# Attention scores over 128 contraction rows, one operand kept per head in tiles whose other 64 rows are zero

## The chip, the cores and the metric

The kernel runs on one core of one Trainium2 chip. Its metric is the device time of one execution in microseconds (us), of which the median of several runs is taken. The engines are named as in the profile: PE (matrix products; PEld is its loading of the stationary operand), DVE (vector), ACT (activation functions and copies), POOL (general vector work beside DVE) and SP (which issues most DMAs).

## The reference

Two layers of a decoder trunk over 512 tokens of 1024 features. Layer 0 mixes with attention, layer 1 with a gated delta rule; each is followed by a gated feed-forward part. The change lies in layer 0, where 8 "moba" heads (softmax) and 8 stick-breaking heads of 64 features share one input projection:

```python
proj = h @ w_in
qa, ka, va, qb, kb, vb = (t.reshape(B, T, -1, HEAD_DIM) for t in jnp.split(proj, cuts, axis=-1))
qa = partial_rope(qa, positions)
ka = partial_rope(ka, positions)
# moba heads: with 512 tokens and blocks of 256 this is causal attention
s = einsum('bhqd,bhkd->bhqk', q, k) * dh ** -0.5;  p = softmax(where(causal, s, -inf));  o = p @ v
# stick-breaking heads
z = einsum('bhqd,bhkd->bhqk', q, k) * dh ** -0.5
log_1m = where(strictly_causal, log_sigmoid(-z), 0)
w = exp(log_sigmoid(z) + reverse_cumsum(log_1m) - log_1m);  o = w @ v
```

## The kernel before

Activations lie with features on the 128 partitions and tokens on the free axis. Every product of float32 numbers is made from two rounded parts, a high one and a low one (`h` and `l` at the end of a tile's name): `split` makes the high part by a copy (on ACT, or POOL for some weights) and the low part by a subtraction (DVE), and a product is three matmuls, high by high, high by low, low by high.

One 128-row projection holds two heads of 64 features, a *pair*: head 0 in partitions 0 to 63, head 1 in 64 to 127. There are four pairs; of each pair `finish` makes `qa`, `ka` (scaled, turned by the rotary tables: a shuffle on DVE, a product with `S` on POOL, two DVE operations, then `split`), `qb` and `kb`. The work of a pair is done head by head, `moba` and `stick` in turn, so there are eight units of work. In a unit each of `moba` and `stick` makes four blocks of scores, of 128, 256, 384 and 512 columns, each by one call of `qk3`:

```python
PE.matmul(ps, kh[rs, ks], qh[rs, qs], start=True, stop=False)
PE.matmul(ps, kh[rs, ks], ql[rs, qs], start=False, stop=False)
PE.matmul(ps[:, at], e.identb, mask, start=False, stop=False)
steps[-1].append(PE.matmul(ps, kl[rs, ks], qh[rs, qs], start=False, stop=True).ins)
```

`rs` is the head's 64 partitions, so the three score matmuls contract over 64 rows; the mask in bf16 contracts over 128. `moba` passes q where this text has k and the other way round, so its stationary operand is `qa`; that of `stick` is `kb`. Behind the scores of `moba` come a maximum, an exponential, a scaling, four transposes on PE, a split, and the product with v (`pv_out`); behind those of `stick` three ACT functions, a split, products with triangular constants (`ntri`, `nones`), an exponential, a split on POOL, and `pv_out`.

PE takes its work in a fixed order. While the heads of a pair go on, the projections of the next pair (`proj`, and `vproj` for v) fill PE between their steps: `spread` hands each part of a projection a score matmul behind which it is issued. The order on each engine is found when the kernel is built, and each engine then keeps it.

The attention begins with a stage in which the first projections go along with the arrival of the normed input, chunk by chunk (the loop over `k`): loads of two blocks of `ada_w` (tile `aw`, from the pool `rtmp`, 6 buffers), their product with `cond` on DVE, the norm, one weight load (`raw`), its split, and 24 matmuls. The rotary tables are made in it on POOL. In the attention 24 more products `aw` run on POOL (`AENG`), each followed by a sum on ACT; they hang on nothing but their loads and two buffers. The pool `sq0` of `start()` holds the squares of the input before that loop.

Of the kernel before, what the change touches and what calls it, by code (L numbers as in the profile page):

```python
# [8 lines left out]
F32 = mybir.dt.float32  # L9
# [8 lines left out]
T = 512  # L18
# [112 lines left out]
def build(nc, tc, I, O):  # L131
# [3 lines left out]
    with ctx:  # L135
# [40 lines left out]
        crow = apool.tile([1, D], F32, name="crow")  # L176
        nc.scalar.dma_start(crow, I["c"])
        load_x(xctx.enter_context(pool("xp0", "right")), I["x"], nc.sync)
# [74 lines left out]
        # all weights in the order of their use; the loads and splits run ahead of it  # L253
# [12 lines left out]
        def fetch():  # L266
# [3 lines left out]
            if keep == "h":  # L270
                # in the place of h, which is used no more
# [71 lines left out]
        def start():  # L343
            """cond, and rstd of the first norm."""
# [45 lines left out]
        def out_proj(chunk_w, o, layer, gate, nsplit, after, order=None, between=None, halves=HALVES, keep=False):  # L390
            """x += gate * (w^T o), the last chunks by halves of the tokens; after(half) follows each half."""
# [23 lines left out]
        def halves_first(keys, banks, hs, keep):  # L415
            """Products of some chunks of weights by halves of the tokens, into banks."""
# [93 lines left out]
def attention(e, x0ctx):  # L510
    nc, tc, V, G, A, PE, I = e.nc, e.tc, e.V, e.G, e.A, e.PE, e.I
    from contextlib import ExitStack
    with ExitStack() as ctx:
        p1 = ctx.enter_context(e.pool("at1"))
        # rotary tables
# [8 lines left out]
        def rotary():  # L524
            """cos and -sin, sin of the angles: one frequency and 32 positions to a partition, then spread."""
# [42 lines left out]
        # v by kind and pair of heads; a pair's outputs take the place of the v of the pair before  # L568
# [6 lines left out]
        ctx2 = ExitStack()  # L575
        qk = ctx2.enter_context(e.pool("qk"))
        fin = ctx2.enter_context(e.pool("afin"))

        def finish(ps, name, scale, rope):
            h = qk.tile([128, T], F32R, name=name + "h", bufs=1)  # L580
            l = qk.tile([128, T], F32R, name=name + "l", bufs=1)
            if rope:
                q = fin.tile([128, T], F32, name="rq", bufs=2)
                A.activation(q, ps, AF.Copy, scale=scale)
                sw = fin.tile([128, T], F32, name="rs", bufs=1)
                V.stream_shuffle(sw, q, swap)
                G.tensor_tensor(sw, sw, S, op=OP.mult)
                V.tensor_tensor(q, q, C, op=OP.mult)
                V.tensor_tensor(q, q, sw, op=OP.add)
                e.split(q, h, l)  # L590
            elif scale != 1.0:
                A.activation(h, ps, AF.Copy, scale=scale)
                V.scalar_tensor_tensor(l, ps, scale, h.bitcast(F32), op0=OP.mult, op1=OP.subtract)
            else:
                e.split(ps, h, l)
            return h, l

        KINDS = (("qa", 0.125, True), ("ka", 1.0, True), ("qb", 0.125, False), ("kb", 1.0, False))

        # the first projections go along with the arrival of h, chunk of features by chunk  # L600
        with e.psum_pool("start") as sp, e.pool("rtmp") as tmp:
            pq = [sp.tile([128, T], F32, name=f"pq{i}") if i < 1 else e.mm_tile() for i in range(4)]
            pv = [sp.tile([128, T], F32, name=f"pv{i}") for i in range(4)]
            for k in range(KC):
                for comp in (1, 0):
                    with tc.issue_after(first[0]):
                        e.ada(0, comp, k, tmp, 6)
                    e.ada_fin1(0, comp, e.gmix if comp == 1 else None, k)
                e.ahead[0] = AHEAD if k == KC - 1 else 0
                with tc.issue_after(first[1]):  # L610
                    wh, wl = e.load_w(("attn_first", k))
                ins = e.norm_h(FULL, 0, 0, 1, hs, (k,))
                if k == 0:
                    first = (ins.ins, first[1])
                xh, xl = hs[k]
                a, z = k == 0, k == KC - 1
                if k == ROT:
                  with tc.issue_after(e.pins[0]):
                    nc.sync.dma_start(e.call, I["consts"])
                    rotary()  # L620
                for i in range(4):
                    PE.matmul(pq[i], wh[:, i], xh, start=a, stop=False)
                    PE.matmul(pq[i], wh[:, i], xl, start=False, stop=False)
                    PE.matmul(pq[i], wl[:, i], xh, start=False, stop=z)
                vwh = wh[:, 4:].rearrange("p a b -> p (a b)")
                vwl = wl[:, 4:].rearrange("p a b -> p (a b)")
                for c in range(4):
# [4 lines left out]
            with tc.issue_after(sin[0].ins):  # L632
                e.act_set()
# [635 lines left out]
```

## Time and profile before

| | |
|---|---|
| three runs | 1464.26, 1464.52 (median), 1466.06 us |
| profiled execution, span from its first to its last instruction | 1463.8 us |
| busy share of the span | PE 97%, PEld 81%, DVE 60%, ACT 40%, POOL 27% |
| first loop over `k` | about 18 to 71 us |
| attention units, from the first score product on | 86.8 to about 312 us |
| feed-forward of layer 0, delta rule, feed-forward of layer 1 | the rest |

What lies around the span is not measured apart; the median of the runs stands 0.7 us above the span. A matmul's end is modelled in the profile, so PE reads as busy almost everywhere; what it costs is read from the distance between the starts of one matmul and the next. "Busy" on the other engines can be taken as it stands.

### The profile page before, as it was taken

Reading aid. Unit: us, or ns where it says so; the run is one execution under the profiler, and the core shown is the slowest. Engines: PE = TensorE matmul, PEld = TensorE weight load, DVE = VectorE, ACT = ScalarE, POOL = GpSimd, SP = SyncE. Lnnn points to the kernel's source line nnn. Section 1 sums busy time; section 2 is a strip of 40 time slices with the busy share of each in tenths; the row PEclk is TensorE's granted clock in tenths of the full one; section 3 lists DMA queues with packets and bytes.
Section 4 is the critical chain, followed back from the end, with each engine's and each line's share of the span. In section 5 each row is a group of like instructions: output and inputs, shape, how many; then the busy total and the mean of one; then the engine's idle time right before and its main releaser. Section 6 shows DMA issues by size and latency. Waiting matters only on the chain.

```text
span 1463.8 us, 19775 instructions
## 1 busy us (share of the span) xinstructions
PE 1416.0 (97%) x7610; PEld 1188.0 (81%) x7610; DVE 879.6 (60%) x1408; ACT 581.6 (40%) x1133; POOL 395.4 (27%) x360
## 2 busy tenths in 40 slices
PE   8889999999999999999999999999999999999997
PEld 4677677769888888888978777999998888888887
DVE  7588875656566666523677888757784343333233
ACT  4466555664322222222446643345563222222222
POOL 2868833212211111001334644432112000000010
PEclk9999999999999999999999999999999999999999
DMA  9444420123266776633632223223262323233332
GB/s 371 149 159 140 155 71 16 44 85 106 83 235 216 247 237 216 197 110 115 186 95 76 68 74 104 80 78 115 91 206 65 101 94 95 100 101 94 90 96 80
DMA packets 57007, 184.44 MB, mean 126 GB/s; under 512 B 6761, under 2 KB 11113, under 8 KB 56914
## 3 DMA queue, kind: packets, MB, share of 16 engines
q1 hardware_dynamic: 55104, 179.91, 37.7%
q0 software_dynamic: 656, 2.23, 0.7%
q8 instruction: 59, 0.97, 0.3%
q10 hardware_dynamic: 1154, 1.05, 0.2%
q14 instruction: 34, 0.28, 0.1%
HBM read 177.88 MB, written 5.29 MB: 125 GB/s over the span
## 4 chain that ended last, share of the span: by engine, by line
PE 66%; DVE 6%; ACT 2%; DMA 2%; issue 2%; POOL 1%; DVEq 0%; ACTq 0%; POOLq 0%
PE mm L309 18%; PE mm L310 18%; PE mm L311 18%; PE mm L1076 1%; PE mm L1077 1%; PE mm L1075 1%; DMA vp<-dr 1%; DVE vp L972 1%; PE f L309 1%; PE f L310 1%; DVE wl L250 1%; PE f L311 1%; PE bank L910 1%; DVE sq L374 1%; DMA raw<-in_ffn_in_dram 1%
## 5 line engine op out<-in xcount | busy, mean ns | idle before, releaser
L245 ACT ACTIVATE wh<-raw 128x1024 fp32r<-128x1024 f32 (+1 forms) x199 | 206.7, 1040 | 516.6 <-PE mm L310 384.8
L250 DVE TENSOR_TENSOR wl<-raw,wh 128x1024 fp32r<-128x1024 f32 (+1 forms) x205 | 270.1, 1319 | 213.6 <-ACT wh L245 200.1
L309 PE MATMUL mm<-hh,wh 128*128 128x512 f32 (+1 forms) x776 | 295.7, 381 | 2.4 <-DVE acc L863 2.4
L311 PE MATMUL mm<-hh,wl 128*128 128x512 f32 (+1 forms) x776 | 291.5, 377 | 1.2 <-DVE wl L250 1.2
L310 PE MATMUL mm<-hl,wh 128*128 128x512 f32 (+1 forms) x776 | 292.3, 377 | 0.0
L309 PEld LDWEIGHTS mm<-hh,wh 128*128 128x128 f32 x776 | 147.4, 190 | 30.7 <-issue 2.8
L311 PEld LDWEIGHTS mm<-hh,wl 128*128 128x128 f32 x776 | 147.4, 190 | 27.5 <-DVE wl L250 1.8
L310 PEld LDWEIGHTS mm<-hl,wh 128*128 128x128 f32 x776 | 147.5, 190 | 24.1
L247 POOL TENSOR_SCALAR ah<-ac 128x512 fp32r<-128x512 f32 x36 | 40.6, 1129 | 336.8 <-DVE ac L471 336.8
L311 PE MATMUL mm<-ah,wl 128*128 128x512 f32 (+1 forms) x354 | 126.4, 357 | 1.2 <-DVE wl L250 1.2
L309 PE MATMUL mm<-ah,wh 128*128 128x512 f32 (+1 forms) x354 | 126.3, 357 | 0.1
L310 PE MATMUL mm<-al,wh 128*128 128x512 f32 (+1 forms) x354 | 126.0, 356 | 0.0
L309 PE MATMUL mm<-h1h,wh 128*128 128x512 f32 x320 | 124.5, 389 | 0.0
L310 PE MATMUL mm<-h1l,wh 128*128 128x512 f32 x320 | 124.5, 389 | 0.0
L311 PE MATMUL mm<-h1h,wl 128*128 128x512 f32 x320 | 124.5, 389 | 0.0
L471 DVE TENSOR_TENSOR ac<-sg,mm 128x512 f32<-128x512 f32 x40 | 27.5, 688 | 129.1 <-PE mm L311 129.1
L213 DVE CUSTOM_DVE_ANT_0 aw<-aw,cond 128x1024 f32<-128x1024 f32 x72 | 94.7, 1339 | 6.1 <-DMA aw<-in_ada_w_dram 6.0
L329 POOL TENSOR_TENSOR ssq<-ssq,sq 128x512 f32<-128x512 f32 x14 | 22.1, 1577 | 210.3 <-ACT sq L325 210.3
L311 PEld LDWEIGHTS mm<-ah,wl 128*128 128x128 f32 x354 | 66.9, 189 | 11.1 <-DVE wl L250 1.6
L309 PEld LDWEIGHTS mm<-ah,wh 128*128 128x128 f32 x354 | 66.8, 189 | 10.4 <-issue 0.5
L310 PEld LDWEIGHTS mm<-al,wh 128*128 128x128 f32 x354 | 66.9, 189 | 9.4 <-issue 0.2
L310 PEld LDWEIGHTS mm<-h1l,wh 128*128 128x128 f32 x320 | 60.1, 188 | 12.5
(403 smaller groups left out, 2805.1 us busy)
## 6 DMA issues: line engine op xcount, KB each, us to landing
aw<-in_ada_w_dram SPq DMA_DIRECT2D x96, 512.0 KB
raw<-in_ffn_in_dram SPq DMA_DIRECT2D x88, 512.0 KB
raw<-in_ffn_out_dram SPq DMA_DIRECT2D x36, 512.0 KB
raw<-in_gdn_in_dram SPq DMA_DIRECT2D x26, 512.0 KB
raw<-in_gdn_z_dram SPq DMA_DIRECT2D x16, 512.0 KB
raw<-in_gdn_out_dram SPq DMA_DIRECT2D x16, 512.0 KB
raw<-in_ffn_out_dram SPq DMA_DIRECT2D x18, 384.0 KB
raw<-in_attn_in_dram SPq DMA_DIRECT2D x12, 512.0 KB
```

Source lines behind the costliest of these rows:

```text
L213: return V.tensor_tensor_reduce(w, w, cond, 1.0, 0.0, OP.mult, OP.add, mod[:, j:j + 1])
L245: ins = A.activation(h, src, AF.Copy)
L247: G.tensor_scalar(h, src, 1.0, 1.0, op0=OP.mult, op1=OP.mult)
L250: (G if eng == "p" else V).tensor_tensor(l, src, h.bitcast(F32), op=OP.subtract)
L309: PE.matmul(ps, wh[k][:, 0], xh[:, cs], start=first and k == order[0], stop=False)
L310: PE.matmul(ps, wh[k][:, 0], xl[:, cs], start=False, stop=False)
L311: PE.matmul(ps, wl[k][:, 0], xh[:, cs], start=False, stop=last and k == order[-1])
L329: eng.tensor_tensor(ssq[:, cs], ssq[:, cs], sq[:, cs], op=OP.add)
L374: ins = V.scalar_tensor_tensor(t[:, cs], x, modcol(layer, scale, k), rstd[:, cs], op0=OP.mult, op1=OP.mult)
L471: ins = V.tensor_tensor(ac, sg, pu, op=OP.mult)
L910: PE.matmul(ps[:, c], lhs[:, cs], rhs[:, cs], start=True, stop=True)
L972: V.tensor_tensor(DV[:, :m, m:], DV[:, :m, m:], d, op=OP.subtract)
```

## The change

`qa` and `kb`, the two stationary operands of the score products, are kept in tiles of their own for each head. A tile has 128 rows; 64 of them hold the head, the other 64 are set to zero once by POOL, eight tiles in all. The score products then read all 128 rows of both operands: the other head's rows of the moving side meet zeros. `finish` splits `qa` and `kb` in two halves of 64 rows (`finish_apart`), two copies and two subtractions where there was one of each. To make room, the pools `qk` and `fin` are opened after `rtmp` is closed, so `rtmp` now lies where `sq0` was; `crow` goes into the pool of the input; and `w` of `stick` takes one of the three buffers `sq`.

```diff
-        crow = apool.tile([1, D], F32, name="crow")
+        xp0 = xctx.enter_context(pool("xp0", "right"))
+        crow = xp0.tile([1, D], F32, name="crow")
...
         ctx2 = ExitStack()
-        qk = ctx2.enter_context(e.pool("qk"))
-        fin = ctx2.enter_context(e.pool("afin"))
...
-        with e.psum_pool("start") as sp, e.pool("rtmp") as tmp:
+        with e.psum_pool("start") as sp:
             pq = [sp.tile([128, T], F32, name=f"pq{i}") if i < 1 else e.mm_tile() for i in range(4)]
             pv = [sp.tile([128, T], F32, name=f"pv{i}") for i in range(4)]
+            with e.pool("rtmp") as tmp:
+                for k in range(KC):
...
+            qk = ctx2.enter_context(e.pool("qk"))
+            fin = ctx2.enter_context(e.pool("afin"))
+            apart = {}
+            for name in ("qa", "kb"):
+                for head in range(2):
+                    apart[name, head] = [qk.tile([128, T], F32R, name=f"{name}{part}{head}", bufs=1) for part in "hl"]
+                    for t in apart[name, head]:
+                        G.memset(t[64 * (1 - head):64 * (2 - head)].bitcast(F32), 0.0)
+
+            def finish_apart(src, name, scale):
+                for head in range(2):
+                    rs = slice(64 * head, 64 * head + 64)
+                    h, l = (t[rs] for t in apart[name, head])
+                    e.split(src[rs], h, l)
+                return [apart[name, head] for head in range(2)]
...
+                if (name, 0) in apart and not rope:
+                    return finish_apart(ps, name, scale)
...
+                    if (name, 0) in apart:
+                        return finish_apart(q, name, scale)
                     e.split(q, h, l)
...
-            PE.matmul(ps, kh[rs, ks], qh[rs, qs], start=True, stop=False)
-            PE.matmul(ps, kh[rs, ks], ql[rs, qs], start=False, stop=False)
+            PE.matmul(ps, kh[:, ks], qh[:, qs], start=True, stop=False)
+            PE.matmul(ps, kh[:, ks], ql[:, qs], start=False, stop=False)
             PE.matmul(ps[:, at], e.identb, mask, start=False, stop=False)
-            steps[-1].append(PE.matmul(ps, kl[rs, ks], qh[rs, qs], start=False, stop=True).ins)
+            steps[-1].append(PE.matmul(ps, kl[:, ks], qh[:, qs], start=False, stop=True).ins)
...
-                qk3(s[:, :n], q, qs, k, slice(0, n), rs, qs, causal)
+                qk3(s[:, :n], q[h], qs, k, slice(0, n), qs, causal)
...
-                w = work.tile([128, T], F32, name="w", tag="w", bufs=2)
+                w = e.wpool.tile([128, T], F32, name="sq", tag="sq", bufs=3)
```

The built order moves too, on every engine up to the end of the attention; behind it all five engines have the rows that they had. Three places matter below.

SP, the first loads behind those of the input (`call` is the table of constants). Before:

```order
L208 DMA aw<-in_ada_w_dram 128x1024 x2
L269 DMA raw<-in_attn_first_dram 128x1024
L208 DMA aw<-in_ada_w_dram 128x1024 x2
L269 DMA raw<-in_attn_first_dram 128x1024
L208 DMA aw<-in_ada_w_dram 128x1024 x2
L269 DMA raw<-in_attn_first_dram 128x1024
L619 DMA call<-in_consts_dram 128x1025
```

and now:

```order
L270 DMA raw<-in_attn_first_dram 128x1024 x3
L599 DMA call<-in_consts_dram 128x1025
L209 DMA aw<-in_ada_w_dram 128x1024 x6
L270 DMA raw<-in_attn_first_dram 128x1024
```

Three weight loads and the constants have moved ahead of the first `aw`, which now waits for PE to have read the squares in whose place it lies.

POOL, behind the making of the rotary tables (`rs` is the rotary product of `qa`, then of `ka`, of the first pair). Before:

```order
L210 TENSOR_TENSOR aw<-aw,cond 128x1024 x2
L587 TENSOR_TENSOR rs<-rs,S 128x512
L210 TENSOR_TENSOR aw<-aw,cond 128x1024 x2
L587 TENSOR_TENSOR rs<-rs,S 128x512
L210 TENSOR_TENSOR aw<-aw,cond 128x1024 x3
```

and now, behind two `aw` products as before:

```order
L623 MEMSET qah_611 64x512
L623 MEMSET qal_612 64x512
L623 MEMSET qah_615 64x512
L623 MEMSET qal_616 64x512
L623 MEMSET kbh_619 64x512
L623 MEMSET kbl_620 64x512
L623 MEMSET kbh_623 64x512
L623 MEMSET kbl_624 64x512
L211 TENSOR_TENSOR aw<-aw,cond 128x1024 x2
L644 TENSOR_TENSOR rs<-rs,S 128x512
L211 TENSOR_TENSOR aw<-aw,cond 128x1024
L644 TENSOR_TENSOR rs<-rs,S 128x512
```

Eight fillings with zeros and two `aw` products have come ahead of the first rotary product.

ACT, at the end of the first loop, where `qa`, `ka`, `qb` and `kb` of the first pair are read out of PSUM (two `rq`, `qbh`, `kbh`). Before:

```order
L245 ACTIVATE wh<-raw 128x1024
L211 ACTIVATE aw,mod<-aw 128x1024 x2
L245 ACTIVATE wh<-raw 128x1024
L584 ACTIVATE rq<-pq_206 128x512
L584 ACTIVATE rq<-mm 128x512
L592 ACTIVATE qbh<-mm 128x512
```

and now:

```order
L246 ACTIVATE wh<-raw 128x1024
L212 ACTIVATE aw,mod<-aw 128x1024 x2
L246 ACTIVATE wh<-raw 128x1024 x2
L641 ACTIVATE rq<-pq_197 128x512
L212 ACTIVATE aw,mod<-aw 128x1024
L641 ACTIVATE rq<-mm 128x512
L651 ACTIVATE qbh<-mm 128x512
```

One more weight copy stands ahead of the first read, and the sum of a third `aw` product between the first read and the second.

## Rows read from the trace of the kernel before

**Rows 1.** The page: the span, and the busy time, share and number of instructions of each engine, and what the DMA engines moved in each of 40 equal slices of the span (36.6 us each).

```profile
span 1463.8 us, 19775 instructions
PE 1416.0 (97%) x7610; PEld 1188.0 (81%) x7610; DVE 879.6 (60%) x1408; ACT 581.6 (40%) x1133; POOL 395.4 (27%) x360
...
GB/s 371 149 159 140 155 71 16 44 85 106 83 235 216 247 237 216 197 110 115 186 95 76 68 74 104 80 78 115 91 206 65 101 94 95 100 101 94 90 96 80
```

**Rows 2.** Busy time by stretch: start and end of the stretch, its length, then busy time and number of instructions of PE, PEld, DVE, ACT, POOL, the granted clock of PE as a share of 2.4 GHz, the DMA share and GB/s.

```profile
72.00:87.00 15.00, 11.18 (x74) 10.53 (x74) 14.97 (x33) 9.07 (x30) 9.48 (x5) 0.89 0.53 187
87.00:189.00 102.00, 98.14 (x506) 73.95 (x506) 87.00 (x120) 66.11 (x162) 81.68 (x51) 1.00 0.46 150
189.00:302.00 113.00, 113.00 (x540) 81.52 (x538) 72.52 (x144) 64.88 (x157) 32.53 (x39) 1.00 0.10 33
```

**Rows 3.** PE in order of time (start and duration in us, line, tiles, contraction rows * stationary columns, shape of the moving side): a score product of 128 columns, one of 512, and what stands before and behind them.

```profile
224.07 0.39 PE L754 MATMUL z<-ssl,ntri 128*128 128x512 f32 x1
224.38 0.32 PE L697 MATMUL z<-qbh,kbh 64*128 64x128 f32 x1
224.55 0.27 PE L698 MATMUL z<-qbl,kbh 64*128 64x128 f32 x1
224.75 0.23 PE L699 MATMUL z<-strictT,identb 128*128 128x128 bf16 x1
224.91 0.32 PE L700 MATMUL z<-qbh,kbl 64*128 64x128 f32 x1
225.16 0.50 PE L309 MATMUL mm<-hh,wh 128*128 128x512 f32 x1
...
226.41 0.40 PE L310 MATMUL mm<-hl,wh 128*128 128x512 f32 x1
226.74 0.50 PE L697 MATMUL s<-kah,qah 64*128 64x512 f32 x1
227.08 0.39 PE L698 MATMUL s<-kal,qah 64*128 64x512 f32 x1
227.40 0.23 PE L699 MATMUL s<-causal,identb 128*128 128x128 bf16 x1
227.56 0.49 PE L700 MATMUL s<-kah,qal 64*128 64x512 f32 x1
227.99 0.50 PE L309 MATMUL mm<-hh,wh 128*128 128x512 f32 x1
```

**Rows 4.** The same view a little earlier: matmuls of 128 contraction rows one behind the other, of 512, 384, 256 and 128 columns.

```profile
222.80 0.39 PE L311 MATMUL mm<-hh,wl 128*128 128x512 f32 x1
223.03 0.34 PE L754 MATMUL z<-ssh,nones 128*128 128x384 f32 x1
223.21 0.33 PE L754 MATMUL z<-ssl,nones 128*128 128x384 f32 x1
223.38 0.28 PE L754 MATMUL z<-ssh,nones 128*128 128x256 f32 x1
223.50 0.28 PE L754 MATMUL z<-ssl,nones 128*128 128x256 f32 x1
223.61 0.22 PE L754 MATMUL z<-ssh,nones 128*128 128x128 f32 x1
223.67 0.27 PE L754 MATMUL z<-ssl,nones 128*128 128x128 f32 x1
223.78 0.45 PE L754 MATMUL z<-ssh,ntri 128*128 128x512 f32 x1
```

**Rows 5.** The instructions of line 697 (the first matmul of every score product) in the stretch 87 to 189: number, shortest, median and longest duration in ns, first and last start, shapes.

```profile
L697 PE MATMUL s<-kah,qah x14: 302/384/497, 86.8 to 187.4; 64*128 64x128 f32 x4, 64*128 64x256 f32 x4, 64*128 64x384 f32 x3, 64*128 64x512 f32 x3
L697 PE MATMUL z<-qbh,kbh x12: 271/409/497, 87.5 to 180.3; 64*128 64x128 f32 x3, 64*128 64x256 f32 x3, 64*128 64x384 f32 x3, 64*128 64x512 f32 x3
```

**Rows 6.** Groups of instructions by line in the stretch 86 to 189 (number | busy us, mean ns of one | idle before): a split of 64 rows by 512 columns, on ACT and on DVE.

```profile
L245 ACT ACTIVATE ah-1_174<-o 64x512 fp32r<-64x512 f32 x2 | 1.2, 594 | 0.7 <-PE o L690 0.6
L250 DVE TENSOR_TENSOR bl-1_185<-o,bh-1_184 64x512 fp32r<-64x512 f32 x2 | 1.4, 686 | 0.0
```

**Rows 7.** POOL: the one filling of a tile of 512 columns (line 518, durations in ns), then its instructions in order of time between 63 and 87 us.

```profile
L518 POOL MEMSET C<- x1: 543/543/543, 2.2 to 2.2; 128x512 f32 x1
...
63.28 5.71 POOL L210 TENSOR_TENSOR aw<-aw,cond 128x1024 f32<-128x1024 f32 x2
73.13 1.78 POOL L587 TENSOR_TENSOR rs<-rs,S 128x512 f32<-128x512 f32 x1 [4.14 <-DMA aw<-in_ada_w_dram]
80.01 2.27 POOL L587 TENSOR_TENSOR rs<-rs,S 128x512 f32<-128x512 f32 x1
```

**Rows 8.** ACT and PE in order of time at the end of the first loop and before the first score product (idle time before, and what ended it, in brackets).

```profile
69.02 1.06 ACT L211 ACTIVATE aw<-aw 128x1024 f32<-128x1024 f32 x1 [2.18 <-POOL aw L210]
71.50 0.59 ACT L584 ACTIVATE rq<-mm 128x512 f32<-128x512 f32 x1
...
72.14 0.38 PE L676 MATMUL mm<-wh,hh 128*128 128x256 f32 x1 [0.93 <-ACT rq L584]
81.18 0.38 PE L677 MATMUL mm<-wl,hh 128*128 128x256 f32 x1 [3.25 <-DVE wl L250]
86.80 0.33 PE L697 MATMUL s<-kah,qah 64*128 64x128 f32 x1
```

**Rows 9.** SP in order of time: it issues the first two loads of `aw`.

```profile
4.70 1.09 SPq L208 DMA_DIRECT2D aw<-in_ada_w_dram  x2
```

More of the change, by code (lines that the diff above doesn't have):

```diff
@@ L573, in vtile @@
             return [t.rearrange("p (c f) -> p c f", c=4) for t in store[kind, p]]
+        KINDS = (("qa", 0.125, True), ("ka", 1.0, True), ("qb", 0.125, False), ("kb", 1.0, False))
         ctx2 = ExitStack()
-        qk = ctx2.enter_context(e.pool("qk"))
-        fin = ctx2.enter_context(e.pool("afin"))
[L579 to L596, printed above, removed]
@@ L598, in attention @@
-        KINDS = (("qa", 0.125, True), ("ka", 1.0, True), ("qb", 0.125, False), ("kb", 1.0, False))
-        with e.psum_pool("start") as sp, e.pool("rtmp") as tmp:
+        with e.psum_pool("start") as sp:
             pq = [sp.tile([128, T], F32, name=f"pq{i}") if i < 1 else e.mm_tile() for i in range(4)]
             pv = [sp.tile([128, T], F32, name=f"pv{i}") for i in range(4)]
[L604 to L627, printed above, removed]
-                    t = slice(c * 128, c * 128 + 128)
-                    PE.matmul(pv[c], xh[:, t], vwh, start=a, stop=False)
-                    PE.matmul(pv[c], xh[:, t], vwl, start=False, stop=False)
-                    PE.matmul(pv[c], xl[:, t], vwh, start=False, stop=z)
-            with tc.issue_after(sin[0].ins):
-                e.act_set()
@@ new lines, in attention @@
+            with e.pool("rtmp") as tmp:
+                for k in range(KC):
+                    for comp in (1, 0):
+                        with tc.issue_after(first[0]):
+                            e.ada(0, comp, k, tmp, 6)
+                        e.ada_fin1(0, comp, e.gmix if comp == 1 else None, k)
+                    e.ahead[0] = AHEAD if k == KC - 1 else 0
+                    with tc.issue_after(first[1]):
+                        wh, wl = e.load_w(("attn_first", k))
+                    ins = e.norm_h(FULL, 0, 0, 1, hs, (k,))
+                    if k == 0:
+                        first = (ins.ins, first[1])
+                    xh, xl = hs[k]
+                    a, z = k == 0, k == KC - 1
+                    if k == ROT:
+                      with tc.issue_after(e.pins[0]):
+                        nc.sync.dma_start(e.call, I["consts"])
+                        rotary()
+                    for i in range(4):
+                        PE.matmul(pq[i], wh[:, i], xh, start=a, stop=False)
+                        PE.matmul(pq[i], wh[:, i], xl, start=False, stop=False)
+                        PE.matmul(pq[i], wl[:, i], xh, start=False, stop=z)
+                    vwh = wh[:, 4:].rearrange("p a b -> p (a b)")
+                    vwl = wl[:, 4:].rearrange("p a b -> p (a b)")
+                    for c in range(4):
+                        t = slice(c * 128, c * 128 + 128)
+                        PE.matmul(pv[c], xh[:, t], vwh, start=a, stop=False)
+                        PE.matmul(pv[c], xh[:, t], vwl, start=False, stop=False)
+                        PE.matmul(pv[c], xl[:, t], vwh, start=False, stop=z)
+                with tc.issue_after(sin[0].ins):
+                    e.act_set()
@@ new lines, in finish @@
+            def finish(ps, name, scale, rope):
+                if (name, 0) in apart and not rope:
+                    assert scale == 1.0
+                    return finish_apart(ps, name, scale)
+                if (name, 0) not in apart:
+                    h = qk.tile([128, T], F32R, name=name + "h", bufs=1)
+                    l = qk.tile([128, T], F32R, name=name + "l", bufs=1)
+                if rope:
+                    q = fin.tile([128, T], F32, name="rq", bufs=2)
+                    A.activation(q, ps, AF.Copy, scale=scale)
+                    sw = fin.tile([128, T], F32, name="rs", bufs=1)
+                    V.stream_shuffle(sw, q, swap)
+                    G.tensor_tensor(sw, sw, S, op=OP.mult)
+                    V.tensor_tensor(q, q, C, op=OP.mult)
+                    V.tensor_tensor(q, q, sw, op=OP.add)
+                    if (name, 0) in apart:
+                        return finish_apart(q, name, scale)
+                    e.split(q, h, l)
+                elif scale != 1.0:
+                    A.activation(h, ps, AF.Copy, scale=scale)
+                    V.scalar_tensor_tensor(l, ps, scale, h.bitcast(F32), op0=OP.mult, op1=OP.subtract)
+                else:
+                    e.split(ps, h, l)
+                return h, l
@@ L728, in stick @@
         def stick(pair, h, q, k):
-            rs = slice(h * 64, h * 64 + 64)
             off = {3: 0, 2: 128, 1: 384, 0: 768}
```

7 lines of the change are left out of this document (3 added, 4 removed).

## The prediction

> **What bounds the kernel now.** I read the page first: PE is busy 97% of 1463.8 us [rows 1], so only what PE does or waits for can move the time. Behind the attention no engine's order changes, so the change must show before about 312 us. I then cut the attention into stretches [rows 2]. From 189 to 302 PE is busy in all of its 113 us, DVE in 72.5, ACT in 64.9 and POOL in 32.5: here PE alone sets the pace. From 87 to 189 PE is busy 98.1 of 102 us, but DVE is at 87.0 (85%) and POOL at 81.7 (80%): PE sets the pace there too, with little room behind it. From 72 to 87 it is the other way round: DVE 14.97 of 15.0, PE 11.2.
>
> Busy says little of PE, so the price of a score product is read from the starts in the timeline [rows 3]. The product of 512 columns begins at 226.74 and the next matmul behind it at 227.99: 1.25 us. The matmul ahead of it, 512 columns at full depth, began at 226.41, so 0.33 us passed before the first score matmul could start. Full-depth matmuls behind one another [rows 4] start 0.23 us apart at 512 columns (222.80 to 223.03), 0.17 to 0.18 at 384, 0.11 to 0.12 at 256, and 0.06 to 0.11 at 128. So a 64-row matmul of 512 columns holds PE for 0.32 to 0.34 us where one of 128 rows holds it for 0.23; the mask of 128 columns between them takes 0.16; the last one 0.43; and entry costs 0.10.
>
> **The change, part by part.**
>
> *Score products.* If they behave like the other 128-row matmuls, one of 512 columns costs 3 x 0.23 + 0.11 for the mask = 0.80 us, against 1.25 + 0.10 = 1.35: 0.55 saved. One of 128 columns goes from 224.38 to 225.16, 0.78, with an entry of 0.31 - 0.23 = 0.08, 0.86 in all; as 128-row work 4 x 0.11 = 0.44: 0.42 saved. I take the mean, 0.485, for the sizes between. Eight units make 2 x 4 products each, 64 in all: 31.0 us of PE. Of these, 14 + 12 = 26 stand between 87 and 189 [rows 5]: 12.6 us there, 18.4 behind it for the other 38. No row shows a product over zeros; the bounds are nothing (the time goes with something other than the 64 rows) and 31.0 us. I take the upper one for PE, because the excess appears at each of the four places where a 64-row matmul stands beside another matmul and nowhere in the full-depth rows.
>
> Here a rule speaks against the change. The Trainium skill, "TensorE: Matmul & The Clock Gate", section "Why this matters for your kernels", says that a single matmul of few contraction rows takes the same time as one of 128, the gain lying only in running several row tiles at once. By that rule padding would save nothing. The rows differ: 0.33 against 0.23 us at 512 columns, and no two score matmuls run at once. The measurement decides for me, and the rule is kept as a rival.
>
> *What the other engines let through.* Between 87 and 189 DVE needs its 87.0 us, plus the second subtraction of `qa` and of `kb` for one pair, 2 x 0.69 [rows 6]: 88.4. Were all of the 12.6 us gained, DVE would be busy 88.4 of 89.4, which in a chain of waits from engine to engine I don't believe; nothing gained is the other end. I take 4 us, which puts DVE at 88.4 / 98 = 90%. Behind 189 the full gain leaves DVE at (72.5 + 2.8) / (113 - 18.4) = 80%, less than it bears in the first stretch now. In that stretch PE is idle 102 - 98.1 = 3.9 us; I take as much off here: 14.4 of 18.4 us. Bounds: 9 (half lost) and 18.4. Together 18.4 us.
>
> *The extra splits* on ACT, 0.59 us each and two for a pair [rows 6], lie beside PE: ACT is at 65% and 57% in the two stretches [rows 2]. Without that cover all eight would cost 4.8 us.
>
> *The start.* The first `aw` loads were issued at 4.70, directly behind the input [rows 9]. Now three weight loads of 512 KB and the constants pass first, 2.1 MB; at the 371 GB/s of the first slice [rows 1] that is 5.7 us, by which the first projection may come later. I count only 1.5 us of it: the weights that pass first are needed too, so what is loaded by the end of the loop is the same, and so is the work of DVE and POOL in it. Bounds 0 and 5.7.
>
> *The zeros.* One filling of 512 columns takes 0.54 us [rows 7], eight 4.3. POOL was idle 4.14 us at just this place, before the first `rs` at 73.13, so the zeros alone would hide. But two `aw` products now stand between them and `rs`, at 5.71 / 2 = 2.9 us each or less. After 63.28 + 5.71 = 69.0 come the zeros to 73.3, then the third `aw` to about 76. ACT, in its order, now sums that third `aw` (1.06 us, as at 69.02) ahead of reading `ka` out of PSUM, which it did at 71.50 [rows 8]. That read now comes near 77. Behind it wait `qb` and `kb` on ACT, and PE, whose first product of `vproj` needs the bank: 72.14 becomes about 77.6. The 3.25 us that PE lost at 81.18 to a late weight split should fall away, since that copy now stands earlier on ACT. Net 2.2; the second `rs`, ending at 82.3 now (80.01 + 2.27), moves to about 84.6 and delays `ka`, and so the first score at 86.80, by as much. I take 2.5 us; bounds 0 and 5.4. The start costs 1.5 + 2.5 = 4 us; its ends are 0 and, since one slip can hide in the other, some 8 rather than 11.1.
>
> The other edits (`crow`, `w` in a buffer of `sq`) add no instruction and give `w` three buffers for two: nothing.
>
> **Sum.** -18.4 + 4 = -14.4 us. Against the profiled execution's span, 1463.8 - 14.4 = 1449.4; the median stands 0.7 us above that span, so 1450.1, said as 1450.
>
> **The rivals.**
>
> *Swallowed.* The first stretch gives nothing, the second half of its 18.4, and the start costs 4 to 8: 1463.8 - 9 + 4 + 0.7 = 1459.5, up to 1463.5. For it: DVE and POOL above 80% in the first stretch, DVE full before it. Against it: the second stretch, where DVE has 40 us to spare and PE none.
>
> *All of it.* Little is lost on the way, 24 to 31 us gained less a start of 0 to 2: 1434 to 1441. For it: the score products are themselves links of the chains that DVE and ACT wait on, so these shorten by about 0.5 us a step as well. Against it: DVE at 99% in the first stretch.
>
> *Slower: the products are no shorter.* The 0.10 to 0.2 us around a score matmul would then belong to its operands or its place between other matmuls, and stay with 128 rows; the start's 4 to 8 us is all that remains: 1468 to 1472. It decides if the step from the first to the second score matmul of 512 columns stays above 0.30 us. The skill's rule above ends here. Against it: 128-row products whose operands are also fresh, and also between others, show none of it [rows 4].
>
> **How the numbers follow.** The forecast, 8 to 23 us gained, 1441 to 1456: 0.66. All of it: 0.08. Swallowed: 0.16, of which 0.06 within 0.2% (2.9 us, about what a measurement of this kernel can tell from no change). Slower: 0.10, of which 0.01 still within it. So faster 0.84, same 0.07, slower 0.09. The range for 8 in 10 takes the forecast, most of the swallowed case and the nearer part of the full one: 1438 to 1462.
>
> **What would show it.** In the profile after, score matmuls of 512 columns should start 0.22 to 0.24 us apart, the mask be followed within 0.12, and entry and exit cost nothing; the chain from the first score to the last block (86.8 to 310 now) should be some 18 us shorter, most of it in the second half; DVE should be busiest between 88 and 180, and PE should wait there for DVE more than now. At the start, PE's first `vproj` matmul should stand near 77 instead of 72.14, behind ACT, and the first score near 90. From about 300 us on, each stage should last as long as before. I am wrong if the steps stay above 0.3 us, if DVE or POOL eats the second half too, or if the start slips by more than 8 us.

## The result, and the profile after

The changed kernel takes 1456.46 us (median of four runs, 1455.33 to 1457.83) against 1465.13 us for the kernel before, timed beside it: a ratio of 0.9946, with a 95% interval of 0.9932 to 0.9960. The profiled execution took 1457.58 us and has a span of 1455.7 us, 8.1 us less than that of [rows 1].

The page of after, as in [rows 1]: span, busy time and share of each engine.

```profile
span 1455.7 us, 19821 instructions
PE 1391.0 (96%) x7610; PEld 1190.6 (82%) x7610; DVE 876.9 (60%) x1416; ACT 584.2 (40%) x1141; POOL 401.1 (28%) x368
```

PE is busy 25.0 us less, but the span is only 8.1 us shorter: 16.9 us of that became time in which PE does nothing. The score products answer to [rows 3]; PE of after in order of time, one product of 512 columns with its neighbours:

```profile
232.26 0.39 PE L312 MATMUL mm<-hh,wl 128*128 128x512 f32 x1
232.49 0.39 PE L721 MATMUL s<-kah,qah 128*128 128x512 f32 x1
232.72 0.39 PE L722 MATMUL s<-kal,qah 128*128 128x512 f32 x1
232.94 0.23 PE L723 MATMUL s<-causal,identb 128*128 128x128 bf16 x1
232.99 0.48 PE L724 MATMUL s<-kah,qal 128*128 128x512 f32 x1
233.30 0.40 PE L310 MATMUL mm<-hh,wh 128*128 128x512 f32 x1
```

Read the starts: 0.23 us to enter, 0.23 from the first to the second score matmul, 0.22 to the mask, 0.05 behind it, 0.31 for the last. From 232.49 to 233.30 are 0.81 us; it was 1.25, and 0.10 for the entry.

Where the 8.1 us come from is best seen with three marks that every kernel here has: the first `vproj` matmul, the last matmul of the last `o`, and the end. Between the first two, PE has the same other work in all of them, so I took the distance from each matmul's start to the next and subtracted its columns at 0.218 us for 512, close to the steps of [rows 4]. Over this stretch the columns alone are 170.4 us in every kernel. What is left is *extra at the scores* (a score matmul or mask is one of the two) or *other waits*, which also hold what a matmul takes longer at a lower clock.

| us | before | after | change | forecast |
|---|---|---|---|---|
| first `vproj` matmul | 72.14 | 83.02 | +10.9 | +4 (as "the start") |
| extra at the scores | 42.8 | 12.5 | -30.3 | -31.0 |
| other waits | 35.7 | 47.9 | +12.2 | +12.6 (31.0 less 18.4) |
| from the last `o` to the end | 1142.9 | 1141.9 | -1.0 | 0 |
| sum | | | -8.2 | -14.4 |

The windows of after, to be held against [rows 2] (columns as there; to the first score, two units, two units, four units):

```profile
83.00:106.00 23.00, 14.91 (x97) 14.15 (x98) 19.42 (x35) 13.79 (x38) 14.74 (x8) 0.87 0.45 139
106.00:168.00 62.00, 56.42 (x327) 48.23 (x327) 50.16 (x76) 40.27 (x102) 50.46 (x32) 0.94 0.50 162
168.00:216.00 48.00, 46.12 (x257) 38.95 (x256) 41.40 (x70) 33.77 (x84) 30.13 (x26) 0.96 0.29 90
216.00:314.00 98.00, 94.14 (x535) 78.15 (x533) 70.45 (x136) 66.54 (x163) 28.92 (x34) 0.99 0.10 32
```

PE now has holes in every stretch, and the granted clock falls below 1.00 in all of them; before, it was 1.00 from 87 to 302 us.

The start, SP of after in order of time, where [rows 9] had the first `aw` at 4.70:

```profile
4.67 1.80 SPq L270 DMA_DIRECT2D raw<-in_attn_first_dram  x3
7.31 0.33 SPq L599 DMA_DIRECT2D call<-in_consts_dram  x1
8.26 8.31 SPq L209 DMA_DIRECT2D aw<-in_ada_w_dram  x6
18.95 0.33 SPq L270 DMA_DIRECT2D raw<-in_attn_first_dram  x1
...
22.37 15.50 SPq L209 DMA_DIRECT2D aw<-in_ada_w_dram  x8
38.68 0.33 SPq L270 DMA_DIRECT2D raw<-in_attn_first_dram  x1
...
45.76 6.01 SPq L270 DMA_DIRECT2D raw<-in_attn_first_dram  x2
```

Six `aw` are issued in one go of 8.31 us, of which SP waits 5.1 us for PE's product of the squares in whose place they lie. Then eight more take 15.50 us, of which most is waiting for buffers, and the weights of the loop's later chunks stand behind them: the last two are issued from 45.76 us on (37.66 before). The first projection slips from 17.80 to 24.12 us (+6.3), the first `vproj` by 10.9.

### The profile page after: what moved, and what is told of

Read it like the earlier page. It is cut to its first block, busy times and chain, and to the rows that moved or that the text cites. A ratio compares the mean times of both kernels' runs of the same rounds, so it can differ in the third digit from the quotient of the medians.

```text
span 1455.7 us, 19821 instructions
## 1 busy us (share of the span) xinstructions
PE 1391.0 (96%) x7610; PEld 1190.6 (82%) x7610; DVE 876.9 (60%) x1416; ACT 584.2 (40%) x1141; POOL 401.1 (28%) x368
## 4 chain that ended last, share of the span: by engine, by line
PE 76%; DVE 10%; POOL 4%; DMA 4%; ACT 3%; issue 2%; SPq 0%; DVEq 0%; POOLq 0%; ACTq 0%
PE mm L310 19%; PE mm L312 19%; PE mm L311 19%; DMA aw<-in_ada_w_dram 2%; DVE wl L251 1%; POOL aw L211 1%; DVE vp L994 1%; PE mm L1098 1%; PE mm L1099 1%; PE mm L1097 1%; PE z L776 1%; DMA vp<-dr 1%; PE f L310 1%; PE f L311 1%; PE f L312 1%
## 5 line engine op out<-in xcount | busy, mean ns | idle before, releaser
L251 DVE TENSOR_TENSOR wl<-raw,wh 128x1024 fp32r<-128x1024 f32 (+1 forms) x205 | 263.6, 1287 | 220.9 <-ACT wh L246 208.0
L251 POOL TENSOR_TENSOR wl<-raw,wh 128x1024 fp32r<-128x1024 f32 x24 | 58.9, 2453 | 44.4 <-ACT wh L246 44.1
```

The source lines that it names most:

```text
L251: (G if eng == "p" else V).tensor_tensor(l, src, h.bitcast(F32), op=OP.subtract)
```

## The experiments

The kernel before, timed beside them, had medians of 1465.5 to 1465.7 us. Marks, waits and clock are those of one profiled execution of each kernel.

**e1_pools_only**: the change without its padding. The pools and the load order are the change's; `qa` and `kb` are split whole, no zeros, scores over 64 rows.

```diff
-            for name in ("qa", "kb"):
-                for head in range(2):
-                    apart[name, head] = [...]   # and the zeros
-            PE.matmul(ps, kh[:, ks], qh[:, qs], start=True, stop=False)
+            PE.matmul(ps, kh[rs, ks], qh[rs, qs], start=True, stop=False)
```

> The places of the tiles and the order of the loads are those of the change; the score products, the splits and the tiles of q and k are those of before (64 rows, no zeros). Theory (the 19 us that the change loses ahead of the first score come from the aw loads, which wait where the squares lie): the first score comes 14 to 19 us later than 86.8, and nothing brings them back: 1477 to 1484 us. Rival 1 (the zeros and the extra splits make the delay): first score within 4 us of 86.8, 1463 to 1469. Rival 2 (late work is caught up behind the first score, because POOL's products and the loads go on while PE waits): first score 14 to 19 us late, but the end only 4 to 10 late: 1469 to 1475.

Measured: 1489.94 us (1487.53 to 1490.51), ratio 1.0167 (1.0151 to 1.0183). The first `vproj` stands at 81.88 us and the other waits at 47.0 us. The first score, at 104.38 us, is as late as the theory had it, but the time is 6 us above its range: the waits behind it are new too. So the late start and the waits come without zeros, split by heads or padding, with the places of the pools and the order built for them; the padding then takes 33.5 us off (1489.94 to 1456.46).

**e2_squares_kept**: the change, with the pool of the squares held open to the end of the first loop, so that `rtmp` gets other space and the first `aw` wait for nothing.

```diff
-            with pool("sq0") as sp:
+            sp = sqctx.enter_context(pool("sq0"))
...
+            e.sqctx.close()
```

> The change, with the pool of the squares held open until the loop over k is done, so that the aw loads no longer lie in its place; the zeros are written where the change writes them. Theory (loads): the first projection is back near 17.8 and the first score at 87 to 92; the 27 us that the change gains behind the first score stay: 1438 to 1444 us. Rival 1 (zeros): first score still 10 us or more late, 1450 to 1457. Rival 2 (part of the 27 us was catching up): first score early, but 1445 to 1450.

Measured: 1451.33 us (1447.59 to 1453.52), ratio 0.9898 (0.9875 to 0.9921). The first `vproj` is back at 71.34 us, the first score stands at 94.23.

**e3_zeros_early**: the change, with the eight tiles in a pool of their own opened ahead of the loop, where the squares were, and filled there.

```diff
+        qz = ctx2.enter_context(e.pool("qz"))
+        ...  apart[name, head] = [qz.tile(...)], G.memset(...)   # moved here
         with e.psum_pool("start") as sp:
```

> As the run with the squares kept, but the eight tiles with zeros have a pool of their own where the squares lay, and are filled by POOL before its first norm, where it is idle. Theory: the zeros cost little where they were, 1 to 3 us less than the run with the squares kept: 1436 to 1442 us. Rival (the zeros are on the path of the first rotary product): 4 to 6 us less than it.

Measured: 1451.14 us (1447.27 to 1454.91), ratio 0.9905 (0.9881 to 0.9930). First `vproj` at 73.12, first score at 91.68 (106 in the change). Both runs show that the place of `rtmp`, and the load order with it, cost the change its start; both missed my expectation, because a part came back behind it: from the first `vproj` to the last `o` e2 takes 6.5 us longer than the change (of 11.7 gained at the start), e3 4.4 (of 9.9). Windows of e3 by the same stretches:

```profile
73.00:92.00 19.00, 14.54 (x100) 13.68 (x101) 16.47 (x38) 12.54 (x37) 13.45 (x6) 0.91 0.41 148
92.00:162.00 70.00, 61.10 (x331) 50.65 (x330) 60.33 (x81) 45.14 (x113) 55.61 (x35) 0.90 0.49 158
162.00:209.00 47.00, 45.62 (x245) 37.64 (x245) 37.78 (x64) 29.18 (x73) 30.70 (x23) 0.96 0.31 101
209.00:309.00 100.00, 95.16 (x540) 78.90 (x538) 70.02 (x140) 67.47 (x167) 29.12 (x35) 0.98 0.10 33
```

The hole is in the first two units: PE is idle 8.9 of 70 us there. The zeros, written in e2 where the change writes them and in e3 ahead of the loop, make no difference that can be told: the two runs are 0.2 us apart.

**e4_mask_last**: the kernel before, with the mask behind the three 64-row matmuls instead of between them.

```diff
-            PE.matmul(ps[:, at], e.identb, mask, start=False, stop=False)
-            steps[-1].append(PE.matmul(ps, kl[rs, ks], qh[rs, qs], start=False, stop=True).ins)
+            PE.matmul(ps, kl[rs, ks], qh[rs, qs], start=False, stop=True)
+            steps[-1].append(PE.matmul(ps[:, at], e.identb, mask, ...).ins)
```

> The kernel before, with the 128-row mask behind the three 64-row matmuls of each score product instead of between them. Theory A (each 64-row matmul pays for a load of weights that nothing hides, about 0.10 us, whatever stands beside it, and the last one pays 0.1 more): extras of a product of 512 columns fall from 0.54 to about 0.40, 64 times 0.13 = 8 us: 1456 to 1460 us. Theory B (the cost is the change between 64 and 128 rows, of which two of four go): half of 31 us: 1447 to 1452. Theory C (a 64-row matmul is simply longer, order is nothing): 1462 to 1466.

Measured: 1459.82 us (1458.87 to 1460.91), ratio 0.9964 (0.9951 to 0.9977). PE in order of time, a product of 512 columns:

```profile
223.00 0.40 PE L310 MATMUL mm<-hl,wh 128*128 128x512 f32 x1
223.32 0.49 PE L697 MATMUL s<-kah,qah 64*128 64x512 f32 x1
223.66 0.39 PE L698 MATMUL s<-kal,qah 64*128 64x512 f32 x1
223.89 0.39 PE L699 MATMUL s<-kah,qal 64*128 64x512 f32 x1
224.22 0.23 PE L700 MATMUL s<-causal,identb 128*128 128x128 bf16 x1
224.25 0.47 PE L309 MATMUL mm<-hh,wh 128*128 128x512 f32 x1
```

From the second to the third 64-row matmul it is 0.23 us, as at full depth; 0.32 on entry, 0.34 from the first to the second, 0.33 from the third to the mask. So 64 rows as such are not dear: two of the dear steps are changes of depth, the third stands directly behind one, and with the mask in the middle there are two such changes more. The weight loads (PEld) of the same product show what differs:

```profile
223.32 0.18 PEld L697 LDWEIGHTS s<-kah,qah 64*128 64x128 f32 x1 [0.37 <-ACT u L747]
223.43 0.19 PEld L698 LDWEIGHTS s<-kal,qah 64*128 64x128 f32 x1
223.66 0.18 PEld L699 LDWEIGHTS s<-kah,qal 64*128 64x128 f32 x1
224.21 0.10 PEld L700 LDWEIGHTS <-identb 128*128 128x128 bf16 x1 [0.36 <-issue]
```

Between equal depths the load starts ahead of its matmul, here by 0.23 us (223.43 for 223.66); at a change of depth it starts only with it, 0.01 us ahead or less (223.32, 224.21). That holds for every change of depth from 86 to 315 us, 132 in this run and 250 in before: at most 5 ns ahead, against some 230 between full-depth matmuls of 512 columns. Why the load comes late there no run shows.

The time lies in theory A's range, but the saving on PE is nearer theory B's: a product of 512 columns with its entry falls from 1.35 to 1.02 us, by 0.33, where A had some 0.14. Over the stage the extra at the scores falls by 18 us (42.8 to 24.8), but the other waits rise by 11.6 (35.7 to 47.3), with the tiles of before.

**e6_early_64**: e3 without zeros and with the 64 rows; `qa` and `kb` still split by heads.

```diff
-                for t in apart[name, head]:
-                    G.memset(t[64 * (1 - head):64 * (2 - head)].bitcast(F32), 0.0)
-            PE.matmul(ps, kh[:, ks], qh[:, qs], start=True, stop=False)
+            PE.matmul(ps, kh[rs, ks], qh[rs, qs], start=True, stop=False)
```

> The places of e3 (the pool of the eight tiles where the squares were, ada_w loaded first), but without zeros, and with the score products over 64 rows as before; only what the places and the split by heads cost is left. Theory: in e3 the two terms of the forecast hold apart (start +4, score products -18), so without the padding the kernel should stand at the time of before plus the start: 1467 to 1472. Rival (the padding is worth the whole 31 us wherever the places are those of the change, as between e1 and the change, 33.5 us): 1480 to 1486. Second rival (the places of e3 cost nothing, its start slips by the zeros alone): 1463 to 1467.

Measured: 1479.49 us (1475.44 to 1481.26), ratio 1.0092 (1.0072 to 1.0111). It is nearest the first rival: the padding is worth 28.4 us here, nearly all of what PE saves, and the rearrangement costs 14 us though its start is in time (first `vproj` 71.32): the other waits are 51.9 us. Where they lie, in us (two units begin with the first score product of `moba` in them):

| other waits | before | after | e3 | e6 | e4 |
|---|---|---|---|---|---|
| first `vproj` to first score | 6.6 | 12.3 | 8.0 | 12.1 | 6.6 |
| units 0, 1 | 9.9 | 13.8 | 20.8 | 12.9 | 16.1 |
| units 2, 3 | 5.4 | 6.9 | 5.8 | 5.0 | 6.9 |
| units 4, 5 | 4.8 | 4.8 | 5.4 | 7.0 | 5.4 |
| units 6, 7 | 8.8 | 10.2 | 10.2 | 14.9 | 12.3 |

**e13_early_unsplit**: e6 with `qa` and `kb` split whole, in four tiles instead of eight.

```diff
-                return [apart[name, head] for head in range(2)]
+        tiles = {name: [qz.tile(...) for part in "hl"] for name in ("qa", "kb")}
```

> e6 (places of e3, 64-row scores, 1479.5 us) without the split by heads: qa and kb are each split whole, one copy and one subtraction as before. The forecast put the extra splits at nothing beside PE, 4.8 us if nothing covers them. If they are the cause of the 14 us that e6 lost: 1465 to 1468. If they cost their uncovered price: 1474 to 1476. If the cause is the other places of the tiles and the order that follows from them on PE: 1477 to 1482.

Measured: 1487.87 us (1487.26 to 1489.03), ratio 1.0149 (1.0134 to 1.0164). It did not test what it was made for: the smaller pool leaves part of the squares' place to `rtmp`, and the start is late again (first `vproj` at 80.65). Only the stretch behind can be used: 263.3 us from the first `vproj` to the last `o`, 266.1 in e6. If the order does the rest alike, the split by heads costs no more than these 2.8 us.

**e12_w_in_sq**: the kernel before, with `w` in a buffer of `sq`.

```diff
-                w = work.tile([128, T], F32, name="w", tag="w", bufs=2)
+                w = e.wpool.tile([128, T], F32, name="sq", tag="sq", bufs=3)
```

> The kernel before with one small part of the change: w of stick takes one of the three buffers sq instead of its own two. The forecast put this at nothing. Theory (nothing): 1463 to 1467. Rival (the shared buffers make ACT or POOL wait, and are part of the 14 us that the rearrangement costs without the padding): 1468 to 1475.

Measured: 1464.81 us, ratio 0.9993 (0.9984 to 1.0002). Nothing, as forecast.

**e7_aw_spread, e8_aw_spread_before, e9_aw_spread_after**: one constant, in e3, in before and in the change.

```diff
-ADA = (6, 6, 6, 6, 0, 0, 0, 0)
+ADA = (3, 3, 3, 3, 3, 3, 3, 3)
```

> e3, with the 24 products aw of the attention handed out three to each of the eight units instead of six to each of the first four. In e3 PE waits for DVE between 108 and 196 us and its clock falls with the waits, while POOL is busy 80% and two thirds of that are these products; behind 196 POOL is at a third. Theory (the first half of the attention is held back by POOL and by what DVE and ACT wait on it for, so it swallows most of its 12.6 us): 1443 to 1448, the slip of the first stretch gone and the second stretch nearly as long as in e3. Rival A (DVE alone holds it back, its work is not moved): 1449.5 to 1452.5. Rival B (the products, put into the second half, hold that back instead): 1452 to 1458.

> The kernel before, with the products aw handed out three to a unit in the same way. There PE is busy 98.1 of the 102 us of the first half. Theory (POOL holds back only once the score products are short): at most the 3.9 us in which PE is idle, 1462 to 1465. Rival (these products cost time in any order): 1455 to 1460. Rival (they do harm in the second half): 1466 to 1470.

> The changed kernel, with the products aw handed out three to a unit. Two of them stand ahead of the first rotary product on POOL, and the late start packs the rest closer. Theory: three fewer stand early, so the first score comes earlier than 106 us, and the first half waits less: 1446 to 1452. Rival A (the late loads of the loop decide, and the first half catches up as much without this): 1455 to 1458. Rival B (the second half is held back): 1458 to 1464.

Measured: 1450.44 us (ratio 0.9897, 0.9882 to 0.9912), 1465.03 (0.9994, 0.9985 to 1.0004) and 1455.34 (0.9933, 0.9917 to 0.9950): each as its parent. They decide nothing, because the edit did not move the work to the later units. The 24 products on POOL in e7, with shortest, median and longest duration and the first and last start:

```profile
L211 POOL TENSOR_TENSOR aw<-aw,cond x24: 2340/2401/3399, 62.6 to 177.1; 128x1024 f32<-128x1024 f32 x24
```

In e3 they began between 64.3 and 175.2. They hang on nothing but loads and buffers, so the built order put them as early as before. That the times of e7 and e9 lie in the ranges of their rivals A says nothing for these.

**e10_dve_relieved, e11_dve_relieved_before**: e7 and e8, with the projection weights of the attention split on ACT and POOL.

```diff
-EA, EVA = 12 * 'g', 'aa'
+EA, EVA = 12 * 'p', 'aa'
```

> The run with aw spread over all units on e3's places, and besides the low parts of the twelve projection weights of the attention subtracted on POOL instead of DVE, and their high parts copied on ACT instead of POOL. This takes 12 subtractions of about 1.3 us from DVE, eight of them from its busiest stretch (about 10 us of 88), and puts them where three aw products a unit left room. Theory (DVE, not POOL, holds the first half back once the score products are short): 1443 to 1448, some of the 12 us regained that PE waits more than before between the first vproj and the third unit. Rival A (the waits come from the order of PE, not from DVE's load): 1449 to 1452. Rival B (POOL's subtractions are slow and late, PE waits for wl from POOL): 1453 to 1460.

> The same relief of DVE (and the same spread of aw) in the kernel before, whose score products contract over 64 rows and whose PE waits little in the first half. Theory: within 2 us of before, 1463 to 1467. If DVE's relief were worth as much here as in the run beside it, the theory would fall: it would be worth 3 to 6 us in any kernel, 1459 to 1462. Rival (POOL late): 1468 to 1475.

Measured: 1451.16 us (ratio 0.9900, 0.9885 to 0.9914) and 1473.07 (1.0058, 1.0036 to 1.0080). DVE is busy 39.1 of the 50 us from 110 to 160, where e3 has 44.6, and in sum nothing is gained: the other waits fall to 46.2 us, the extra at the scores rises to 19.2. But the sum hides two effects. In units 0 and 1 the other waits fall from 20.9 us in e7 to 12.6, as the theory had it; in units 2 and 3 they rise from 4.6 to 9.3, and the extra at the scores there from 3.9 to 8.4. In before the same edit costs 7.4 us, as its last rival had it. So the time is that of rival A, but the run does not decide between DVE's work and the order of PE, which moved with it.

## Why the forecast was right in its range and wrong in a term

The forecast was 1450 us, in a range of 1438 to 1462. Measured were 1456.46 us, inside it, and at the upper edge of the forecast's own main case (1441 to 1456).

*Score products: right.* The forecast was 31.0 us of PE; measured 30.3 between before and after, and with the pools in the same places 33.5 us of the whole time (e1 to after) and 28.4 (e6 to e3). The steps stand where it said: 0.22 to 0.23 apart, the mask 0.05. The rule weighed there (the Trainium skill, "TensorE: Matmul & The Clock Gate", section "Why this matters for your kernels") agrees with one step only, the 0.23 us between two 64-row matmuls in e4; the measurement decides, since a step into, out of or directly behind a change of depth is dearer (0.32 to 0.34 us).

*"The excess appears at each of the four places where a 64-row matmul stands beside another matmul": not quite.* e4 shows two 64-row matmuls in a row without it.

*What the other engines let through: right in size by luck, wrong in reason.* The forecast lost 12.6 of 31.0 us, 8.6 before 189 us and 4 behind; measured +12.2, by the table under e6 some 11 up to the end of unit 3 (near 216 us) and 1 behind. It called this the price of shorter products beside a DVE at 85%. But e1 and e6 have the long products and other waits as large (47.0 and 51.9 us), so the waits come with the rearrangement. On the other hand e4, with the tiles of before, loses 11.6 of 18 us, so shorter products in the old arrangement do meet waits. What they share is open (below).

*The start: the term that failed.* "I count only 1.5 us of it: the weights that pass first are needed too, so what is loaded by the end of the loop is the same". It was 6.3 at the first projection, above the upper end of 5.7, and 10.9 at the first `vproj`, beyond the 8 us that the forecast named as a sign of being wrong. Two things were left out: all six `aw` wait for the squares, not only for 2.1 MB ahead of them, and on SP's queue the later weight loads then stand behind `aw` that wait for buffers. Together they are the 6.9 us between the forecast's +4 and +10.9; how these divide was not measured. The sum missed by 6.2. e2 and e3 take the wait for the squares away (the built order moves with it), and the first `vproj` stands at 71.34 and 73.12 us, 72.14 before. Their times, 14.2 and 14.4 us below before, are the forecast's -14.4, but by luck: the terms of e3 are +1.0 at the start, -28.3 at the scores and +14.6 in other waits, those of the forecast +4, -31.0 and +12.6.

The 2.5 us that the forecast gave to the zeros and the order of ACT are not seen either: with the zeros where the change writes them, e2 has its first `vproj` 0.8 us ahead of before. Its first score, at 94.23 us, is late, but so is that of e6 (94.16), which writes no zeros.

*The first `vproj` behind ACT, near 77.6.* Right in kind, the time is the loop's. ACT of after:

```profile
81.34 1.06 ACT L212 ACTIVATE aw<-aw 128x1024 f32<-128x1024 f32 x1 [1.74 <-POOL aw L211]
82.39 0.58 ACT L641 ACTIVATE rq<-mm 128x512 f32<-128x512 f32 x1
```

It waits 1.74 us for the third `aw` of POOL, sums it, and only then reads `ka`, where [rows 8] had 71.50.

*First score near 90, then 18 us gained, mostly in the second half.* In the change it is 105.96 us, 19.2 later, and 27.3 us come back behind it. The mark was badly chosen: 2.6 us of `vproj` have moved ahead of the first score, and 5.7 us are more waits there. In e3 it is 91.68, and 17.9 us come back.

**What stays open** is what starts the waits in those 12 us. Part of them is not waiting but slower work, which the account of the forecast has no term for. The granted clock of PE has two levels here, 1.00 (2.4 GHz) and 0.50 (1.2 GHz):

```profile
99.90:106.60 6.70, 5.89 (x28) 5.93 (x29) 3.36 (x11) 3.25 (x8) 3.60 (x2) 0.50 0.26 84
```

In after it was 0.50 for 19.4 us between the first `vproj` and the last `o`, in before for 3.4. Matmuls start nearly twice as far apart there (256 columns 0.21 us, at 101.06 and 101.27 below, for 0.12 at the higher level, [rows 4]). From the columns that fell into these times I estimate 7.6 us lost outside the scores, against 1.7 in before: some 6 of the 12.2 us (by the same count 8 of 14.6 in e3, 4 of 11.6 in e4). Each of the five falls between these marks in after stands behind idle time of PE, of 5.88, 2.46, 1.96, 1.88 and 1.35 us. So PE pays twice for a wait, and the question is where the waits come from.

In after the longest wait is before the first score. POOL in order of time:

```profile
87.65 2.65 POOL L211 TENSOR_TENSOR aw<-aw,cond 128x1024 f32<-128x1024 f32 x1 [2.30 <-ACT ah L246]
90.27 1.72 POOL L644 TENSOR_TENSOR rs<-rs,S 128x512 f32<-128x512 f32 x1
91.95 2.40 POOL L211 TENSOR_TENSOR aw<-aw,cond 128x1024 f32<-128x1024 f32 x1
95.14 2.68 POOL L211 TENSOR_TENSOR aw<-aw,cond 128x1024 f32<-128x1024 f32 x1 [0.79 <-DMA aw<-in_ada_w_dram]
```

DVE beside it:

```profile
88.16 2.70 DVE L645 TENSOR_TENSOR rq<-rq,C 128x512 f32<-128x512 f32 x1
90.89 0.69 DVE L251 TENSOR_TENSOR kbl<-mm,kbh 64x512 fp32r<-64x512 f32 x1
91.61 0.49 DVE L251 TENSOR_TENSOR al<-pv,ah 128x128 fp32r<-128x128 f32 x2
92.02 3.59 DVE L251 TENSOR_TENSOR qal<-rq,qah 64x512 fp32r<-64x512 f32 x2
95.85 2.52 DVE L646 TENSOR_TENSOR rq<-rq,rs 128x512 f32<-128x512 f32 x1
98.50 0.27 DVE L251 TENSOR_TENSOR bl<-mm,bh 128x128 fp32r<-128x128 f32 x1
...
100.28 0.27 DVE L251 TENSOR_TENSOR bl<-mm,bh 128x128 fp32r<-128x128 f32 x1
```

PE behind them, products of `vproj` (idle time and its releaser in brackets):

```profile
100.70 0.55 PE L699 MATMUL mm<-wh,hh 128*128 128x256 f32 x1 [5.88 <-DVE bl L251]
101.06 0.41 PE L700 MATMUL mm<-wl,hh 128*128 128x256 f32 x1
101.27 0.41 PE L701 MATMUL mm<-wh,hl 128*128 128x256 f32 x1
```

PE stands still for 5.88 us behind the `bl` subtractions, and these stand behind four DVE instructions, in three rows, that take 8.8 us instead of some 2.8 (0.69 each, as `kbl` shows; `qal` is two). Each overlaps instructions on POOL: the one from 95.14 ends at 97.82, and the DVE instruction from 95.85 ends at 98.37, 0.55 us later. This points to DVE held by POOL as the cause of this wait. That it makes the 12 us is not shown: the last section counts no more of such holding in after than in before, a run that takes POOL's products away was not tried, and e6 to e10 change the place of the waits (the table) more than their sum. The order of PE is the other candidate: in after PE has 83,968 columns of work from the first score product of `moba` in unit 6 to the last `o`, with which to fill the steps of the last two units, in before 97,152.

## What to carry to other kernels

Where a matmul of fewer rows alternates with deep ones, read the starts around it: two neighbours of the same shallow depth can be put together (0.4% here, one line moved) or padded to full depth with zeros on one side (30 us of PE here). When a change moves pools, read who lay in the new place before and which loads on the same queue stand behind the ones that now wait for it; a late start was dearer here (10.9 us) than what could be seen of the zeros (0.2 us) and the splits (2.8 at most). When PE gets holes, read the granted clock behind them as well: here some 6 of 12 us of "waits" were matmuls at the lower level. And see in the order that an experiment moved the work before reading its result.

## What the runs showed of the hardware that was not expected

DVE's busy time in the attention is partly standing still, so it can't be taken as it stands, as it was under the table of before. In the trace of before, 42 of its instructions from 72 to 312 us are more than 1.5 times as long as the short ones of the same line and shape; 39 of them contain the end of a POOL instruction (the three others last 0.015 us; of the 262 that are not stretched 40 do), and the 42 take 46.6 us more than the short ones in all (after: 43, 38 and 42.2 us). How long one is stretched differs, but not where it ends: the 15 stretched ones of 128x512 with two operands in SBUF took 1.02 to 2.74 us in before, and all ended 0.54 to 0.56 us behind the end of a POOL instruction. So part of the 85% of [rows 2], on which a term of the forecast rested, was not work. Groups of DVE in after between 83 and 314 us (busy, mean ns):

```profile
L645 DVE TENSOR_TENSOR rq<-rq,C 128x512 f32<-128x512 f32 x7 | 10.2, 1457 | 0.1
L740 DVE TENSOR_SCALAR p<-p,st 128x384 f32<-128x384 f32 x8 | 9.7, 1219 | 0.2
L740 DVE TENSOR_SCALAR p<-p,st 128x512 f32<-128x512 f32 x8 | 5.2, 656 | 0.2
L770 DVE SCALAR_TENSOR_TENSOR u<-z,u 128x512 f32<-128x512 f32 x8 | 5.5, 683 | 3.4 <-ACT u L769 3.4
L251 DVE TENSOR_TENSOR bl<-mm,bh 128x128 fp32r<-128x128 f32 x16 | 4.5, 280 | 1.7 <-ACT bh L246 1.6
```

A product of two SBUF operands takes 1457 ns on average, one of the same size with an operand in PSUM (`u<-z,u`) 683; the scaling of `p` takes longer at 384 columns than at 512, since more of its instructions were stretched. Of the instructions with an operand in PSUM none was stretched. The Trainium skill, "GPSIMD Engine Reference", section "1. Specifications", says that POOL shares its SBUF interfaces with DVE and contends with instructions of two SBUF inputs or a two-port mode; the trace agrees, with the 39 of 42 above; for the scalings of `p`, which read one tile, it does not show the mode.
